# A streaming encoder step: TensorE's static order worked out with nine of its model's latencies changed

## The chip, the cores and the metric

The kernel runs on one core of a Trainium2 chip. The metric is the device time of one execution in microseconds (us). The kernel before took 1478.51 us in the median of three runs (1473.87 to 1479.91). The engines are named as in the profile: PE is TensorE, DVE is VectorE, ACT is ScalarE, POOL is GpSimd, and SP is SyncE, which starts all the DMAs spoken of here.

## The reference

One layer of a streaming encoder for 1024 prompt rows and 32 sample rows, model width 1024, all in 32-bit floats:

```python
xn = rmsnorm(x, pre_norm_g)
u = xn @ w_in                       # gq gk gv gr gg | dq dk dv dg | ma mb
log_a = log_sigmoid(gr @ gla_w_a2 + gla_b_a) / 16
o_gla, state = gla(gq, gk, gv, log_a)            # 4 heads, gated linear attention with a state
y_gla = (rmsnorm(o_gla) * silu(gg)) @ w_proj_gla
o_diff = diff_attend(rope(dq), rope(dk), dv)     # 8 heads, softmax(q1 k1) - lambda * softmax(q2 k2)
y_diff = (rmsnorm(o_diff) * silu(dg)) @ w_proj_diff
y = x + rmsnorm((sigmoid(ma) * y_gla + sigmoid(mb) * y_diff) @ w_out, post_norm_g)
```

Besides y it returns the new keys, values and GLA states. The prompt rows start from nothing; the sample rows attend to 512 past frames and go on from a given GLA state.

## The kernel before

**Products.** Each 32-bit operand is split into a high and a low part, and a product is three matmuls: high by high, high by low, low by high. The projections are lines 486 to 488 (helper `fill`), 464 to 466 (`proj`) and 1122 to 1124 (`pg_first`).

**Stages, in time.** Norm and value projections (to about 220 us); the GLA stage with 4 heads (to about 560); the difference attention with 8 heads (to about 1177); GLA's output projection (to about 1280); that of the difference attention (to about 1373); the last product with `w_out`.

**The order of the work.** In the GLA stage, the difference stage and GLA's output projection TensorE's order is fixed when the program is built. The class `Order` keeps a clock of its own. Each thread of work yields its next step as (cost, needs, banks): what TensorE spends on it, the events it needs with a latency behind each, and the PSUM banks it takes. The first thread in line whose step is ready by the model goes next; the heads' own work stands first, `fill` last. `fill` yields the projections that later heads need, in steps of two k tiles, six matmuls at a modelled cost of 0.9. `S.mark(event)` notes when something was issued, `S.free(tag, latency)` says when a bank comes free again. The latencies are the table `W`:

```python
    def _ready(self, step):
        _, needs, banks = step
        r = max([self.at.get(e, math.inf) + lat for e, lat in needs], default=0.0)
        for tag in set(banks):
            n = banks.count(tag)
            have = sorted(self.banks[tag])
            r = max(r, have[n - 1] if len(have) >= n else math.inf)
        return r
```

If nothing is ready, the model's clock moves on to the first step that will be. At run time nothing is reordered: TensorE works through the fixed order and waits where a step isn't ready. Some `fill` jobs need a result of the head in work (a GLA head's query job waits for the branch of the head before, its key job for the last key transpose of that head, the gate job for that head's output; in the difference stage the query and key jobs wait for the scores of the head before), so there are places where no fill is to be had. The other engines' orders are made by the scheduler from the order of the code.

**The steps spoken of.** In a GLA head: `ps_a` (L579 to L581, eight chunks in two groups of four, in the one bank of tag t, evicted by DVE at L582); `ps_as` (L588 to L590, the sample rows, evicted at L591); a branch on a flag (L600) that all engines take together; then on DVE L643, L637, L644 and L646, which make the decayed keys; `ps_kt` (L654), which transposes them; `pS` and `po` (L700 to L727), the state and the output of each chunk; L181, L182 (POOL) and L733, which normalise a group's output `o_sb`; `ps_y` (L740), its transposes, two for each group, evicted with the gate into `yt` by DVE at L743, and stored from there by SP (L746). `yt` has one buffer.

```python
                yield 0.11 * n, [(("on", h, grp), W["on"]), (("sg", h, e), W["sg"])], ["t"]
                ps = tbank("ps_y")
                ...
                S.free("t", W["y_t"])
```

In the difference stage: `ps_s` (L906, L907) are the scores, from keys `k` and `kl` whose halves are copied by DMA (L862); `ps_t` (L954) transposes the probabilities, split by ACT (L956) and DVE (L957), and `po` (L967 to L969) multiplies them by the values; for the sample rows `ps_st` (L1029) transposes, evicted by ACT (L1031) and DVE (L1032), `po_s` (L1041, L1042) multiplies and is evicted by ACT (L1043), and `ps_so` (L1052) transposes the result. `ps_t`, `ps_st`, `ps_so` share the one bank of tag t, too.

Of the kernel before, what the change touches and what calls it, by code (L numbers as in the profile page):

```python
# [50 lines left out]

W = {
# [3 lines left out]
    "tr_t": 2.27, "dv": 5.65, "at": 2.45, "pv_o": 1.1, "sdg": 1.84, "sdk": 21.35, "kc": 7.45, "ss_s": 3.69,  # L56
    "sp": 7.1, "st_t": 1.14, "sv": 3.44, "spt": 0.43, "so_o": 3.58, "so": 4.1, "so_t": 0.72, "yg0": 4.48,
    "yg": 1.18, "pg_b": 1.72, "sm": 1.98, "sm_w": 0.00141, "sm_s": 2.25, "p": 2.4, "p_w": 0.00204,
}

# [1264 lines left out]
```

## Time and profile before

| | us |
|---|---|
| median of 3 runs | 1478.51 (1473.87 to 1479.91) |
| the profiled execution's own time | 1477.82 |
| its span, first to last instruction | 1476.1 |
| PE busy | 1422.4 (96%) |
| DVE, ACT, POOL busy | 789.9, 600.5, 300.2 |
| granted clock of TensorE, mean | 0.990 |

The profile is of one execution; what lies between its span and its own time (1.7 us) is start and end. Times in rows are from the start of the span. A bracket at the end of a row of the timeline gives the idle time of the engine before that row and what ended it. Matmuls overlap: their durations are longer than the distance from one to the next, so distances are read from start to start.

### The profile page before, as it was taken

The numbers are of one execution on the slowest core, as the hardware profiler recorded it, in microseconds if no ns is written. First come the engines' busy times: TensorE is split into PE (matmuls) and PEld (weight loads), VectorE is DVE, ScalarE is ACT, GpSimd is POOL, SyncE is SP. The second block draws the span as 40 slices with busy tenths as digits, with TensorE's granted clock in tenths as the row PEclk, the third lists the DMA queues.
The fourth block names the chain that finished last, engine by engine and source line by source line (L and its number), as shares of the span: only waits on it lengthen the run. The fifth ranks groups of instructions, "written<-read, shape, count | busy, mean of one in ns | idle before, by whom it ended". The sixth has DMA issues, their size and how long they took to land.

```text
span 1476.1 us, 22367 instructions
## 1 busy us (share of the span) xinstructions
PE 1422.4 (96%) x8848; PEld 1327.5 (90%) x8848; DVE 789.9 (54%) x1464; ACT 600.5 (41%) x1262; POOL 300.2 (20%) x186
## 2 busy tenths in 40 slices
PE   8999999989999999899999999999899899999997
PEld 6787779889999899899989998998899799999997
DVE  5602005756565343576776766678665536455415
ACT  4513114535354233455555555555455432221311
POOL 1200002222223124223222222222221111122001
PEclk9999999999999999999999999999999999999999
DMA  8620111122222233313232332223222278634205
GB/s 303 211 107 31 45 50 50 54 73 73 87 64 86 71 109 110 98 54 116 68 100 69 97 90 93 75 77 90 92 69 80 96 265 306 222 132 132 101 1 193
DMA packets 66742, 156.58 MB, mean 106 GB/s; under 512 B 10008, under 2 KB 28568, under 8 KB 65600
## 3 DMA queue, kind: packets, MB, share of 16 engines
q1 hardware_dynamic: 66624, 155.01, 32.5%
q8 instruction: 74, 1.21, 0.4%
q14 instruction: 44, 0.36, 0.1%
HBM read 104.39 MB, written 40.04 MB: 98 GB/s over the span
## 4 chain that ended last, share of the span: by engine, by line
PE 51%; DVE 6%; DMA 4%; ACT 2%; issue 1%; POOL 1%; SPq 0%; DVEq 0%; POOLq 0%; ACTq 0%
PE ps_w L486 9%; PE ps_w L487 9%; PE ps_w L488 9%; PE ps_w L465 2%; PE ps_w L464 2%; PE ps_w L466 2%; PE ps_s L907 2%; PE ps_t L954 2%; PE ps_s L906 2%; PE ps_c L1216 2%; PE ps_c L1218 2%; PE ps_c L1217 2%; DMA ydr<-ydd 1%; DMA kl<-kl 1%; PE po L968 1%
## 5 line engine op out<-in xcount | busy, mean ns | idle before, releaser
L486 PE MATMUL ps_w<-X,wh 128*128 128x352 f32 x1344 | 452.5, 337 | 1.4 <-DVE vo L292 1.1
L487 PE MATMUL ps_w<-X,wl 128*128 128x352 f32 x1344 | 437.7, 326 | 0.0
L488 PE MATMUL ps_w<-X,wh 128*128 128x352 f32 x1344 | 435.7, 324 | 0.0
L456 POOL TENSOR_TENSOR wl<-wr,wh 128x1024 fp32r<-128x1024 f32 x72 | 180.5, 2507 | 656.3 <-ACT wh L454 493.1
L486 PEld LDWEIGHTS ps_w<-X,wh 128*128 128x128 f32 x1344 | 255.0, 190 | 5.5 <-issue 3.0
L487 PEld LDWEIGHTS ps_w<-X,wl 128*128 128x128 f32 x1344 | 255.4, 190 | 1.2 <-issue 1.2
L488 PEld LDWEIGHTS ps_w<-X,wh 128*128 128x128 f32 x1344 | 254.7, 190 | 0.0
L912 ACT ACTIVATE p<-ps_s,nm 128x256 f32<-128x256 f32 (+7 forms) x128 | 94.6, 741 | 58.8 <-DVE ps_s L908 30.8
L306 PE MATMUL ps_v<-wh,X 128*128 128x512 f32 x248 | 97.6, 394 | 1.2 <-DVE X L245 1.2
L305 PE MATMUL ps_v<-wh,X 128*128 128x512 f32 x248 | 98.5, 397 | 0.2 <-DVE g L343 0.2
L307 PE MATMUL ps_v<-wl,X 128*128 128x512 f32 x248 | 98.3, 396 | 0.0
L454 ACT ACTIVATE wh<-wr 128x1024 fp32r<-128x1024 f32 x72 | 75.9, 1054 | 54.6 <-PE ps_w L488 30.6
L910 DVE TENSOR_REDUCE nm<-ps_s 128x1 f32<-128x256 f32 (+7 forms) x128 | 94.8, 747 | 2.7
L292 DVE TENSOR_TENSOR vo<-ps_v,vo 32x512 f32<-32x512 f32 x4 | 2.7, 678 | 140.8 <-ACT vo L291 140.8
L908 DVE MEMSET ps_s<- 64x64 f32 x128 | 14.3, 112 | 115.9 <-PE ps_s L907 114.3
L671 POOL TENSOR_TENSOR vl<-vr,vh 128x512 fp32r<-128x512 f32 (+1 forms) x20 | 24.6, 1228 | 219.4 <-ACT vh L670 219.4
L906 PE MATMUL ps_s<-k,q 128*128 128x512 f32 (+2 forms) x192 | 68.0, 362 | 1.2 <-DMA k<-k 1.2
L907 PE MATMUL ps_s<-kl,q 128*128 128x512 f32 (+2 forms) x192 | 63.8, 348 | 3.7 <-DMA kl<-kl 3.7
L288 ACT ACTIVATE vo<-ps_v 128x512 f32<-128x512 f32 x32 | 19.1, 595 | 115.1 <-PE ps_v L307 114.7
L956 ACT ACTIVATE ah<-ps_t 128x512 fp32r<-128x512 f32 (+2 forms) x96 | 46.9, 488 | 43.5 <-PE ps_t L954 42.7
L957 DVE TENSOR_TENSOR al<-ps_t,ah 128x512 fp32r<-128x512 f32 (+2 forms) x96 | 53.2, 554 | 18.3 <-ACT ah L956 17.0
L465 PE MATMUL ps_w<-Y,wl 128*128 128x352 f32 x192 | 62.2, 324 | 0.0
(319 smaller groups left out, 2968.8 us busy)
## 6 DMA issues: line engine op xcount, KB each, us to landing
wr<-w SPq DMA_DIRECT2D x72, 512.0 KB
thd<-gate SPq DMA_DIRECT2D x16, 528.0 KB
xn<-xn SPq DMA_DIRECT2D x16, 512.0 KB
wr<-wv SPq DMA_DIRECT2D x16, 512.0 KB
newk<-rr SPq DMA_DIRECT2D x8, 528.0 KB
ygr<-ygd SPq DMA_DIRECT2D x8, 528.0 KB
tha<-thd SPq DMA_DIRECT2D x8, 528.0 KB
ydr<-ydd SPq DMA_DIRECT2D x8, 528.0 KB
```

Source lines behind the costliest of these rows:

```text
L305: mm(ps, xk[:, 0, t0 : t0 + P], wh[:, k, :], start=(k == 0), stop=False)
L306: mm(ps, xk[:, 1, t0 : t0 + P], wh[:, k, :], start=False, stop=False)
L307: mm(ps, xk[:, 0, t0 : t0 + P], wl[:, k, :], start=False, stop=(k == KT - 1))
L456: nc.gpsimd.tensor_tensor(wl, wr, wh.bitcast(F32), op=ALU.subtract)
L465: mm(ps[:, :n], wl[:, k, :], src[k][:, 0, t0 : t0 + n], start=False, stop=False)
L486: mm(ps[:, :n], wh[:, k, :], src[k][:, 0, t0 : t0 + n], start=(k == 0), stop=False)
L487: mm(ps[:, :n], wl[:, k, :], src[k][:, 0, t0 : t0 + n], start=False, stop=False)
L488: mm(ps[:, :n], wh[:, k, :], src[k][:, 1, t0 : t0 + n], start=False, stop=(k == KT - 1))
L906: mm(ps[:, n0 : n0 + n], qs[m][:, qsl], ks[m][:, n0 : n0 + n], start=True, stop=False)
L907: mm(ps[:, n0 : n0 + n], qs[m][:, qsl], kls[m][:, n0 : n0 + n], start=False, stop=True)
L910: ve.tensor_reduce(nm, ps[:, 0:w], axis=AX.X, op=ALU.max, negate=True)
L912: act(p[:, 0:w], ps[:, 0:w], AF.Exp, bias=nm, accum_out=sm[:, m : m + 1])
```

## The change

Nine latencies of the table `W` get other values. No instruction is added or removed; the same steps come in another order on TensorE, and the other engines' orders follow it.

```diff
-    "a_t": 1.14, "as_t": 0.79, "kd": 3.96, "kt_t": 0.3, "kt": 8.05, "v": 3.97, "s_s": 0.37, "st": 1.91,
-    "po_o": 0.67, "sg": 0.65, "on": 6.76, "y_t": 0.64, "pv": 1.41, "m_o": 1.54, "dq": 7.76, "dk": 14.32,
...
+    "a_t": 2.5, "as_t": 0.79, "kd": 5.6, "kt_t": 0.3, "kt": 8.05, "v": 3.97, "s_s": 0.37, "st": 1.91,
+    "po_o": 0.67, "sg": 0.65, "on": 7.8, "y_t": 1.6, "pv": 1.41, "m_o": 1.54, "dq": 18.0, "dk": 19.0,
...
```

In the two lines left out `tr_t` goes from 2.27 to 2.5, `st_t` from 1.14 to 2.6 and `so` from 4.1 to 4.9. `a_t` is how long the bank is taken behind `ps_a`, `y_t` behind `ps_y`, `tr_t` behind `ps_t`, `st_t` behind `ps_st`; `kd` is from the issue of the decayed keys to `ps_kt`, `on` from that of the normalised output to `ps_y`, `dq` and `dk` from the end of a query or key job to the head's first scores, and `so` from the samples' last scaling to `ps_so`.

Three places in the order. First, TensorE where GLA head 0 ends and head 1 begins (`X_88` are the normed rows that the fill jobs read). Before:

```order
L588 MATMUL ps_as<-qh,kh 32x32
L589 MATMUL ps_as<-qh,kl 32x32
L590 MATMUL ps_as<-ql,kh 32x32
L486 MATMUL ps_w<-X_88,wh 128x352
L487 MATMUL ps_w<-X_88,wl 128x352
L488 MATMUL ps_w<-X_88,wh 128x352
L486 MATMUL ps_w<-X_88,wh 128x352
L487 MATMUL ps_w<-X_88,wl 128x352
L488 MATMUL ps_w<-X_88,wh 128x352
L599 TENSOR_LOAD fl
L600 COMPARE_AND_BRANCH
```

After:

```order
L725 MATMUL po<-sh,qh 128x256
L726 MATMUL po<-sh,ql 128x256
L727 MATMUL po<-sl,qh 128x256
L588 MATMUL ps_as<-qh,kh 32x32
L589 MATMUL ps_as<-qh,kl 32x32
L590 MATMUL ps_as<-ql,kh 32x32
L599 TENSOR_LOAD fl
L600 COMPARE_AND_BRANCH
```

Before, behind the last `po` of head 0 came one fill step, a group of `ps_a`, two fill steps, `ps_as`, one step, the branch, two steps, and both `ps_y`. After, the six steps and the group stand ahead of that `po`; `ps_as` follows it at once, the branch `ps_as`, and both `ps_y` the branch. On DVE L181 and L733 have moved behind the branch.

Second, TensorE at the first scores of the difference stage, a piece of the difference (`+` is what stands there now):

```order
+L486 MATMUL ps_w<-X_88,wh 128x352
+L487 MATMUL ps_w<-X_88,wl 128x352
+L488 MATMUL ps_w<-X_88,wh 128x352
+L486 MATMUL ps_w<-X_88,wh 128x352
+L487 MATMUL ps_w<-X_88,wl 128x352
+L488 MATMUL ps_w<-X_88,wh 128x352
 L906 MATMUL ps_s<-k_6794,q_6600 128x128
 L907 MATMUL ps_s<-kl_6796,q_6600 128x128
```

Up to the first `ps_s` 36 matmuls of fill, six steps, have moved ahead; SP's queue has the copies of `k` and `kl` in the same place between the same transfers as before.

Third, TensorE at the end of the difference stage (`po_s` are the samples' products, `po` the last product with the values). Before, one fill step behind the first `ps_st`:

```order
L486 MATMUL ps_w<-X_89,wh 128x352
L487 MATMUL ps_w<-X_89,wl 128x352
L488 MATMUL ps_w<-X_89,wh 128x352
L1029 MATMUL ps_st<-ident,p 32x128
L1041 MATMUL po_s<-vcs,smp 32x128 x4
L1042 MATMUL po_s<-smp 32x128
L954 MATMUL ps_t<-ident,p 128x128 x8
L1041 MATMUL po_s<-vcs,smp 32x128 x4
L1042 MATMUL po_s<-smp 32x128
L967 MATMUL po<-ah,vh 128x256
L968 MATMUL po<-al,vh 128x256
L969 MATMUL po<-ah,vl 128x256
```

After:

```order
L486 MATMUL ps_w<-X_89,wh 128x352
L487 MATMUL ps_w<-X_89,wl 128x352
L488 MATMUL ps_w<-X_89,wh 128x352
L1029 MATMUL ps_st<-ident,p 128x128 x4
L954 MATMUL ps_t<-ident,p 128x128 x8
L967 MATMUL po<-ah,vh 128x256
L968 MATMUL po<-al,vh 128x256
L969 MATMUL po<-ah,vl 128x256
```

Before, a fill step, the second `ps_st` and the first `po_s` group stood between the first `ps_st` and the last two `ps_t` (one row, x8), and the other `po_s` group between these and `po`. After, `ps_st`, both `ps_t` and `po` follow one another; the second `ps_st` comes behind `po`, and both `po_s` groups and `ps_so` come among the matmuls of GLA's output projection.

Elsewhere on TensorE, counted in the two orders: the first of the three `ps_kt` of a head comes one step later behind `ps_as` (two in head 3), the second `ps_st` of a head pair one step later behind the first, a second `ps_y` one step later behind the first in most groups. The first `ps_y` of head 3's last group comes two steps behind its last `po`, where it came six steps behind. The first `ps_a` group of head 1 comes one fill step, one `po` and two `pS` groups (12 small matmuls) behind head 0's fourth `ps_y`, where two more steps and two more groups of each lay between; that of head 2 comes two steps behind head 1's last big `ps_y`, where it came four steps behind. In head 2 the two `ps_y` of the last group follow each other without a step between, where one lay between, with one step ahead of them behind a `ps_a` group and two steps between them and `ps_as`.

More of the change, by code (lines that the diff above doesn't have):

```diff
@@ L53 @@
     "w_pj": 1.5, "z_s": 6.02, "z": 15.1, "a": 0.07, "pf_t": 0.58, "gk": 0.6, "gq": 4.35, "qk": 8.01,
[2 rows of a table removed]
-    "tr_t": 2.27, "dv": 5.65, "at": 2.45, "pv_o": 1.1, "sdg": 1.84, "sdk": 21.35, "kc": 7.45, "ss_s": 3.69,
-    "sp": 7.1, "st_t": 1.14, "sv": 3.44, "spt": 0.43, "so_o": 3.58, "so": 4.1, "so_t": 0.72, "yg0": 4.48,
[2 rows of a table added]
+    "tr_t": 2.5, "dv": 5.65, "at": 2.45, "pv_o": 1.1, "sdg": 1.84, "sdk": 21.35, "kc": 7.45, "ss_s": 3.69,
+    "sp": 7.1, "st_t": 2.6, "sv": 3.44, "spt": 0.43, "so_o": 3.58, "so": 4.9, "so_t": 0.72, "yg0": 4.48,
     "yg": 1.18, "pg_b": 1.72, "sm": 1.98, "sm_w": 0.00141, "sm_s": 2.25, "p": 2.4, "p_w": 0.00204,
```

## The prediction

> **What bounds the kernel now.** I read the busy shares first, then TensorE's waits, then the timeline around each wait.
>
> ```profile
> span 1476.1 us, 22367 instructions
> PE 1422.4 (96%) x8848; PEld 1327.5 (90%) x8848; DVE 789.9 (54%) x1464; ACT 600.5 (41%) x1262; POOL 300.2 (20%) x186
> ```
>
> TensorE is the bound: 1476.1 − 1422.4 = 53.7 us are idle, and the change removes no matmul. So only idle time and clock can move. The waits of TensorE name the idle time that the nine values could touch (columns: us in total, times, longest):
>
> ```profile
> engine line waited for: us in total, times, longest us
> PE ps_y L740 <- DVE yt L743: 5.2, 4, 2.6
> PE ps_kt L654 <- DVE k L646: 4.5, 3, 2.5
> ...
> PE ps_s L907 <- DMA kl<-kl: 3.7, 4, 2.2
> PE ps_st L1029 <- DVE smp L1032: 3.6, 2, 2.3
> ...
> PE pf L550 <- DVE yt L743: 0.7, 1, 0.7
> ```
>
> Each is a step that the model thought ready and that was not. A longer latency puts fill steps ahead of it. A fill step's price, from TensorE's timeline beside one group of transposes (start, duration, line):
>
> ```profile
> 318.99 0.28 PE L727 MATMUL po<-sl,qh 128*128 128x256 f32 x1
> 319.11 0.32 PE L486 MATMUL ps_w<-X,wh 128*128 128x352 f32 x1
> ...
> 320.07 0.22 PE L579 MATMUL ps_a<-qh,kh 128*128 128x128 f32 x1
> ```
>
> From 319.11 to 320.07 one step of six matmuls: 0.96 us, 0.16 us per matmul.
>
> The long waits cost more than their length. The windows' columns are length, PE, PEld, DVE, ACT and POOL busy (count), granted clock, DMA:
>
> ```profile
> core 0: us, PE busy (x) PEld busy (x) DVE busy (x) ACT busy (x) POOL busy (x), PEclk, DMA share, GB/s
> ...
> 500.00:502.00 2.00, 2.00 (x9) 2.00 (x8) 0.81 (x2) 1.06 (x2) 0.00 (x0) 0.50 0.01 3
> ...
> 600.00:605.00 5.00, 5.00 (x19) 5.00 (x19) 1.16 (x4) 0.46 (x2) 0.00 (x0) 0.51 0.01 4
> 605.00:610.00 5.00, 5.00 (x34) 5.00 (x33) 1.80 (x8) 1.87 (x6) 0.00 (x0) 1.00 0.00 0
> ...
> 1036.00:1040.00 4.00, 4.00 (x17) 3.52 (x17) 0.13 (x2) 0.54 (x1) 0.00 (x0) 0.70 0.43 165
> ```
>
> At 0.51 of the clock 19 matmuls ran in 5 us, at full clock 34: 15 too few, 15 x 0.15 = 2.2 us lost after the stall at 598. By the same rate (6.8 per us) 500–502 lost 4.6 matmuls, 0.7 us, and with what is left of that slow stretch on either side about 1.2; 1036–1040 lost 10, 1.5 us.
>
> **What goes.** The stalled steps, from TensorE's timeline, the idle time before each in brackets:
>
> ```profile
> 400.18 0.66 PE L740 MATMUL ps_y<-ident,o_sb 128*128 128x128 f32 x4 [0.79 <-DVE yt L743]
> 419.18 0.28 PE L654 MATMUL ps_kt<-ident,k 128*32 128x128 f32 x1 [1.25 <-DVE k L646]
> 495.67 0.32 PE L488 MATMUL ps_w<-X,wh 128*128 128x352 f32 x1
> 498.48 0.28 PE L654 MATMUL ps_kt<-ident,k 128*32 128x128 f32 x1 [2.49 <-DVE k L646]
> 595.74 0.30 PE L906 MATMUL ps_s<-k,q 128*128 128x128 f32 x1 [1.16 <-DMA k<-k]
> 598.25 0.44 PE L907 MATMUL ps_s<-kl,q 128*128 128x128 f32 x1 [2.21 <-DMA kl<-kl]
> 599.36 0.45 PE L907 MATMUL ps_s<-kl,q 128*128 128x128 f32 x1 [0.45 <-DMA kl<-kl]
> 1034.82 0.27 PE L1029 MATMUL ps_st<-ident,p 128*32 128x128 f32 x1 [2.31 <-DVE smp L1032]
> ```
>
> - kd 3.96 to 5.6: one step more ahead of the three key transposes that wait, two at the last. The three waits are 4.5 − 1.25 − 2.49 = 0.76, 1.25 and 2.49: off come 0.76, 0.96 and 1.9, and with the last the slow clock, 1.2. Together 4.8.
> - dk, dq: the first scores come six steps, 5.8 us, later. Their copies keep their place on SP's queue, so 1.16 + 2.21 + 0.45 = 3.8 go, and 2.2 of clock: 6.0. The other 1.0 of the 3.7 at L907 are later heads and stay.
> - st_t 1.14 to 2.6: one step more before the second sample transpose: 0.96 of each of the two waits (3.6 − 2.31 = 1.3, and 2.31), and 1.5 of clock: 3.4.
> - y_t 0.64 to 1.6: one step more: 0.79 here and the 0.7 at L550: 1.5.
>
> The gaps are counted from the modelled end of the matmul before; from 495.67 + 0.16 to 498.48 it is 2.65, so each stall that vanishes gives 0.16 more: eight, 1.3. Sum removed: 4.8 + 6.0 + 3.4 + 1.5 + 1.3 = 17.0 us.
>
> **What comes.** Fill is not made, it is moved. Where its next job waits for the head in work, fill runs out, and each step spent earlier is missing there. Three such places are in the order: the change of head 0 to 1, the last group of head 3, and the end of the difference stage.
>
> Head 0 to 1: VectorE's and TensorE's timeline, and a row of the view by source on who waits for the branch (us, times):
>
> ```profile
> 315.33 0.75 DVE L743 SCALAR_TENSOR_TENSOR yt<-ps_y,gg_half,sg 128x512 f32<-128x512 f32 x1 [1.68 <-DMA ygd<-yt]
> 321.15 0.65 DVE L181 TENSOR_SCALAR ss<-ss 128x4 f32<-128x4 f32 x1
> 323.03 1.22 DVE L733 TENSOR_TENSOR o_sb<-o_sb,ss 128x1024 f32<-128x1024 f32 x1 [0.91 <-POOL ss L182]
> 324.91 0.20 PE L588 MATMUL ps_as<-qh,kh 128*32 128x32 f32 x1 [1.42 <-DVE ar L582]
> 328.84 1.23 DVE L643 TENSOR_TENSOR b<-b 128x1024 f32<-128x1024 f32 x1 [3.45 <-DVEq L600]
> 329.99 1.31 DVE L637 TENSOR_TENSOR al<-ar,ah 128x1024 fp32r<-128x1024 f32 x2
> 332.11 1.11 PE L740 MATMUL ps_y<-ident,o_sb 128*128 128x128 f32 x4 [2.65 <-DVE yt L743]
> ...
>   DVE b L643: 9.1, 4
> ```
>
> The last po ended at 319.27 and the second ps_y started at 332.11: 12.84 us, which held six fill steps (5.8) and a group L579–L581 (12 matmuls, 1.3 by the 0.11 to 0.12 us from one small matmul to the next, 318.99 to 319.11). After, those 7.1 us of work stand ahead of po; behind it come only ps_as, the branch L600 and both ps_y. VectorE's chain is then in line. ps_as waits 1.2 to 2.0 for L582 (the 1.42 lies between), its own matmuls and L591 take about 0.5, and the branch holds VectorE 3.45 in this head (two of its four waits leave (9.1 − 6.9)/2 = 1.1 for each of the others). Then L181 (0.65), L643 (1.23), L733 (1.22, moved behind the branch), L637 (1.31) and the eviction L743 (0.75). Together 8.0 to 11.1 us from po to the second ps_y. I take 10.3, the shorter wait and this head's own branch: 10.3 + 7.1 − 12.84 = +4.5 (2.2 to 5.4), and 0.5 for a clock that stays low longer: +5.0.
>
> Last group of head 3:
>
> ```profile
> 529.11 0.28 PE L727 MATMUL po<-sl,qh 128*128 128x256 f32 x1
> 532.22 1.23 DVE L733 TENSOR_TENSOR o_sb<-o_sb,ss 128x1024 f32<-128x1024 f32 x1 [1.19 <-POOL ss L182]
> ```
>
> po ends at 529.39, o_sb is there at 533.45: 4.06 us. Six steps (5.8) covered it; two (1.9) are left: +2.1. A gap of that length is near those that lost the clock: +2.5, up to 3.6 with the 1.5 of the window at 1036.
>
> End of the difference stage:
>
> ```profile
> 1166.85 0.60 PE L1029 MATMUL ps_st<-ident,p 128*128 128x128 f32 x4
> 1167.90 0.42 DVE L1032 TENSOR_TENSOR smp<-ps_st,smp 128x256 f32<-128x256 f32 x1 [1.93 <-ACT smp L1031]
> ...
> 1171.98 0.66 PE L954 MATMUL ps_t<-ident,p 128*128 128x128 f32 x4 [1.41 <-DVE al L957]
> 1174.32 0.39 PE L967 MATMUL po<-ah,vh 128*128 128x256 f32 x1 [0.36 <-ACT os__13014 L1043]
> ```
>
> One fill step, another ps_st and both po_s groups stood between these. After, ps_st, two ps_t and po follow one another. The first ps_t waits for L1032, 1168.32 − 1166.85 less its own 0.4: 1.0; the second 1.41 as now; po for its last split, 1174.32 − 1171.98 − 0.4 = 1.9. That is 4.3 where 1.41 + 0.36 = 1.8 were: +2.5, and as they come within some 6 us, the 1.5 of clock: +4.0 (2.5 to 4.7). The two po_s groups move into the next stage, each with an eviction like the 0.36: +0.5.
>
> Three places lost their distance to the one bank t: the L579 group after head 0's fourth ps_y, the next head's group after its last ps_y, and a pair of ps_y in head 2 that now has no fill between. Their eviction can wait for yt's store, since yt has one buffer:
>
> ```profile
> 309.66 0.66 PE L740 MATMUL ps_y<-ident,o_sb 128*128 128x128 f32 x4
> 402.83 0.75 DVE L743 SCALAR_TENSOR_TENSOR yt<-ps_y,gg_half,sg 128x512 f32<-128x512 f32 x1 [2.70 <-DMA ygd<-yt]
> ```
>
> The first eviction (315.33 + 0.75 = 316.08) ended 5.8 us behind its ps_y (310.32). Now 12 small matmuls and one fill step stand there, 1.4 + 0.96 = 2.4: 0 to 3.4, and I take 1.0, as the store's start shifts too. The second ended 403.58 − 400.84 = 2.74 behind; two steps (1.9) are left: +0.8. In the pair the second would wait 0.79 + 0.96 = 1.75 by the row at 400.18, where (5.2 − 2.65 − 0.79)/2 = 0.88 is waited now: +0.9; ps_as stands two steps behind it, +0.8 by the same 2.74; and the pair's first is one step behind a group L579: with 0.3 for that +2.0 (1 to 4).
>
> Sum added: 5.0 + 2.5 + 4.0 + 0.5 + 1.0 + 0.8 + 2.0 = 15.8 us (7.8 with the low ends: 2.2 + 2.1 + 2.5 + 0 + 0 + 0 + 1.0). Net −1.2 on the profiled execution's own 1477.82, that is 1476.6; the median of three, 1478.51, is 0.7 above it. I say **1476**.
>
> **A rule weighed.** The trace: a gap of 2.31 us at 1034.82 was followed by 1036–1040 at 0.70 of the clock. The Trainium skill, "TensorE: Matmul & The Clock Gate", section "HAM oscillation — how this bites in real kernels", asks for no idle gap of TensorE above about 3.4 us, so a shorter one would be free. The trace differs: it lost 1.5 us behind 2.31. By the rule the 4.9 us of clock that I remove would have been no gain of the longer latencies.
>
> **Rivals.** (a) The run-out places are better covered than I read: the added terms fall at their low ends, 7.8. Then 1477.8 − 17.0 + 7.8 = 1469. For it: the branch took little in the other heads, and bank t often comes free early. Against: the distances in the order are plain, and 4.06 and 5.8 us are in the trace. 0.20.
>
> (b) Slower: the one yt buffer. With pairs of ps_y closer, each second eviction waits for the first's store, the one bank t is held for the 5.8 us seen once, and three groups behind it stall: (5.8 − 2.4) + (5.8 − 1.9) + (5.8 − 1.9) = 11.2 for the 3.8 counted, and 1.5 of clock on each: 1476.6 + 7.4 + 4.5 = 1488. It decides when stores land over 5 us late. For it: stores stand in line with weight loads on SP's one queue. Against: of the eviction waits only one was near that. 0.14.
>
> (c) The clock falls only behind gaps over 3.4 us and the slow stretches came from elsewhere: they stay, 4.9 of the gain go, and with them the 0.4 + 1.5 of clock that I added behind short gaps: 1476.6 + 4.9 − 1.9 = 1480. For it: the stretch at 598 began while copies were still landing. Against: each of the three windows of half clock above begins right behind a stall of over 2.2 us. 0.03. The page named above would have it so.
>
> (d) The stalls are real but their releasers move as far as the steps do, so nothing changes: 1478. For it: the order of VectorE, ACT and SP moves as well. Against: the copies of the first scores are released by their own job. 0.05.
>
> **How the numbers follow.** A measurement of this kernel tells about 0.5% (7.4 us) from no change: below 1471.1 is faster, above 1485.9 slower. My forecast (0.58) nearly cancels and lies within, as do (c) and (d): same 0.66. (a) is faster, 0.20; (b) slower, 0.14. The range: the unknown ends of the added terms reach 8 below and some 9 above: 1467 to 1486.
>
> **What would show it.** Right: no wait at the first scores (L906, L907) nor a slow clock behind them; key transposes waiting under 1 us; ps_y behind the branch of head 1 waiting some 5 to 8 us in all; waits of over 4 us at the end of the difference stage; PE busy near 1420 with idle about 50. Wrong: idle below 45, so that the places of running out were covered; or long waits of L579 behind yt's store.

## The result, and the profile after

The changed kernel takes 1501.68 us in the median of six runs (1500.29 to 1505.67), the kernel before 1477.95 in six (1473.87 to 1480.96): ratio 1.0168, interval 1.0152 to 1.0184, so 23.7 us slower. The prediction said 1476 and 1467 to 1486. One execution of all those spoken of here took far longer than the others of its kernel (2414.38 us, in the kernel with the split ranked higher) and is left out of its time and ratio. Its profiled execution took 1504.91, its span is 27.1 us longer than that of before. First the page of the changed kernel, span and busy shares:

```profile
span 1503.2 us, 22365 instructions
PE 1427.4 (95%) x8848; PEld 1329.3 (88%) x8848; DVE 797.6 (53%) x1464; ACT 592.2 (39%) x1262; POOL 307.0 (20%) x186
```

TensorE is idle for 75.8 us where it was 53.7, and its work takes 5.0 us longer at a mean clock of 0.986 (0.990 before). DVE does the same operations in 7.7 us more; that is the first thing that the prediction had no term for.

TensorE's waits after (us in total, times, longest):

```profile
engine line waited for: us in total, times, longest us
PE ps_y L740 <- DVE o_sb L733: 10.8, 2, 8.6
PE ps_t L954 <- DVE al L957: 9.6, 13, 1.8
PE ps_t L954 <- DVE ps_s L908: 5.2, 4, 2.0
PE ps_t L954 <- DVE p L917: 5.1, 5, 1.5
PE ps_st L1029 <- DVE smp L1032: 4.2, 3, 1.4
PE ps_y L740 <- DVE yt L743: 3.2, 4, 0.8
PE ps_as L588 <- DVE yt L743: 2.7, 1, 2.7
```

The first row holds two places that were foreseen: the change of head 0 to 1 (8.6) and the last group of head 3 (2.2). The three rows of `ps_t`, 19.9 us, 13 + 4 + 5 times, are not in the prediction but for one wait of 1.4 us at the end of the stage. The group of all 288 transposes in the kernel before (busy us, mean ns, then the idle time ahead of them and what ended it):

```profile
L954 PE MATMUL ps_t<-ident,p 128*128 128x128 f32 x288 | 47.6, 274 | 7.0 <-DVE al L957 4.1 <-DVE smp L1055 1.7 <-DVE ps_s L908 0.9
```

After, the same group:

```profile
L954 PE MATMUL ps_t<-ident,p 128*128 128x128 f32 x288 | 48.9, 279 | 21.1 <-DVE al L957 9.6 <-DVE ps_s L908 5.2 <-DVE p L917 5.1
```

The idle time ahead of them has tripled. No row of L906 or L907 is left among the waits.

Where in time: windows cut at the same steps in both kernels (first `ps_z`, last `ps_y`, first `ps_s`, last `po` of the difference stage, first step of the next projection). Columns: length, PE, PEld, DVE, ACT and POOL busy (count), granted clock, DMA share, GB/s. Before:

```profile
core 0: us, PE busy (x) PEld busy (x) DVE busy (x) ACT busy (x) POOL busy (x), PEclk, DMA share, GB/s
...
220.80:552.80 332.00, 315.36 (x2039) 303.29 (x2038) 182.77 (x305) 142.12 (x283) 86.97 (x53) 0.99 0.24 74
552.80:595.70 42.90, 41.79 (x261) 41.48 (x259) 16.73 (x25) 15.95 (x30) 16.32 (x7) 1.00 0.43 129
595.70:1177.30 581.60, 565.78 (x3628) 534.93 (x3628) 394.33 (x781) 300.47 (x692) 139.87 (x66) 0.99 0.28 83
1177.30:1280.00 102.70, 98.29 (x582) 94.39 (x583) 51.60 (x54) 33.11 (x35) 16.96 (x7) 0.98 0.76 268
```

After:

```profile
222.20:565.70 343.50, 319.04 (x2051) 307.22 (x2050) 178.37 (x305) 141.11 (x283) 89.12 (x53) 0.97 0.22 72
565.70:611.20 45.50, 45.50 (x286) 45.50 (x285) 16.72 (x25) 16.39 (x31) 17.27 (x7) 1.00 0.48 142
611.20:1199.60 588.40, 559.42 (x3572) 526.67 (x3571) 410.37 (x778) 292.21 (x686) 143.16 (x64) 0.99 0.27 81
1199.60:1306.10 106.50, 101.05 (x603) 96.22 (x602) 44.32 (x53) 31.78 (x36) 17.39 (x8) 0.98 0.71 250
```

The lengths grow by 11.5, 2.6, 6.8 and 3.8 us; 1.4 and 1.0 lie ahead and behind; together 27.1. But the windows don't hold the same work any more: matmuls have moved over the borders, 12 and 25 into the first two, 21 into the last, 56 out of the difference stage. At the 0.16 us of a matmul that the prediction read, the growth at equal work is 9.6, −1.4, 15.8 and 0.4. So the GLA stage (head 0 to 1, and the rest of its places) lost 9.6, and the difference stage 15.8 although its first stall is gone. In that stage PE's idle time went from 15.8 to 29.0, and DVE was busy 16.0 us longer with three instructions fewer.

### The profile page after: what moved, and what is told of

It is laid out like the page before. It is cut to its first block, busy times and chain, and to the rows that moved or that the text cites. A ratio compares the mean times of both kernels' runs of the same rounds, so it can differ in the third digit from the quotient of the medians.

```text
span 1503.2 us, 22365 instructions
## 1 busy us (share of the span) xinstructions
PE 1427.4 (95%) x8848; PEld 1329.3 (88%) x8848; DVE 797.6 (53%) x1464; ACT 592.2 (39%) x1262; POOL 307.0 (20%) x186
## 5 line engine op out<-in xcount | busy, mean ns | idle before, releaser
L486 PE MATMUL ps_w<-X,wh 128*128 128x352 f32 x1344 | 453.0, 337 | 2.1 <-DVE vo L292 1.1
L456 POOL TENSOR_TENSOR wl<-wr,wh 128x1024 fp32r<-128x1024 f32 x72 | 183.1, 2544 | 527.0 <-ACT wh L454 472.3
L486 PEld LDWEIGHTS ps_w<-X,wh 128*128 128x128 f32 x1344 | 255.2, 190 | 7.2 <-issue 3.3
L908 DVE MEMSET ps_s<- 64x64 f32 x128 | 14.1, 112 | 105.7 <-PE ps_s L907 104.6
L954 PE MATMUL ps_t<-ident,p 128*128 128x128 f32 x288 | 48.9, 279 | 21.1 <-DVE al L957 9.6
L957 DVE TENSOR_TENSOR al<-ps_t,ah 128x512 fp32r<-128x512 f32 (+2 forms) x96 | 53.2, 554 | 29.0 <-ACT ah L956 27.8
L906 PE MATMUL ps_s<-k,q 128*128 128x512 f32 (+2 forms) x192 | 67.6, 360 | 0.0
L956 ACT ACTIVATE ah<-ps_t 128x512 fp32r<-128x512 f32 (+2 forms) x96 | 46.8, 487 | 45.8 <-PE ps_t L954 45.6
L907 PE MATMUL ps_s<-kl,q 128*128 128x512 f32 (+2 forms) x192 | 63.2, 346 | 0.0
```

Source lines behind the costliest of these rows:

```text
L456: nc.gpsimd.tensor_tensor(wl, wr, wh.bitcast(F32), op=ALU.subtract)
L486: mm(ps[:, :n], wh[:, k, :], src[k][:, 0, t0 : t0 + n], start=(k == 0), stop=False)
L906: mm(ps[:, n0 : n0 + n], qs[m][:, qsl], ks[m][:, n0 : n0 + n], start=True, stop=False)
L907: mm(ps[:, n0 : n0 + n], qs[m][:, qsl], kls[m][:, n0 : n0 + n], start=False, stop=True)
```

## The experiments

The theory to test was that the later `dq` and `dk` do the harm. They move the first scores six fill steps back, and by that every head stands at another place against the fill jobs. A job here is twelve steps. Counted in the order, in jobs from its start, the first scores of the eight heads stand at

```
before  24.33  28.50  32.50  36.42  40.42  44.58  48.58  52.50
after   24.83  29.00  33.00  36.92  40.92  44.83  48.83  52.75
```

half a job later for heads 0 to 4, a quarter for the others. What a job asks of the other engines, so the theory, then falls beside other steps of the head: the rotation (L825, L827) and the splitting of the keys (L858, L859) on DVE, the splitting of the weights on POOL (L456). The rivals: bank t, held longer by the model's new `tr_t` and `st_t`; fill that is missing at the end; DVE's queue order by itself, which the scheduler makes anew; and POOL and DVE in each other's way.

### The nine values in three parts

The first kernel is before with `"dq": 18.0, "dk": 19.0` and nothing else.

> The kernel before with dq and dk alone set to 18.0 and 19.0. Theory phase: the six steps ahead of the first scores take away the stall there (7 us), but every later head of the difference stage now stands six steps further along the fill jobs, so POOL's weight split (L456) and the jobs' work on VectorE fall beside the softmax and the transposes: 14 to 17 us more waits at ps_t and po, in all 1484 to 1489. Theory bank (the rival: the new waits at ps_t come from tr_t, st_t and so, which place the transposes and the sample steps): only the stall goes, 1469 to 1473.

Measured 1499.23 against 1478.80, ratio 1.0122 (1.0091 to 1.0152): the sign is the theory's, the size 10 us above its range. The second has the four of the GLA stage alone, `"a_t": 2.5, "kd": 5.6, "on": 7.8, "y_t": 1.6`.

> The kernel before with a_t, kd, on and y_t alone changed. Theory phase: the GLA stage gets about 10 us longer as in the changed kernel, the first scores still stall, and the difference stage, whose order against the fill jobs is that of before, stays within 3 us: 1486 to 1490. Rival (what the GLA stage leaves behind disturbs the difference stage): the 17 us at ps_t come too, 1500 to 1506.

Measured 1489.31, ratio 1.0068 (1.0049 to 1.0088). The third has the rest, `"tr_t": 2.5, "st_t": 2.6, "so": 4.9`.

> The kernel before with tr_t, st_t and so alone changed. Theory phase: the end of the difference stage is 4 us longer, GLA's output projection 2, the two sample waits 3 shorter; the heads are shifted by at most two steps, so that up to 6 us come at ps_t: 1480 to 1487. Theory bank: most of the 17 us at ps_t are here: 1495 to 1499.

Measured 1476.45, ratio 0.9984 (0.9970 to 0.9998), below what was expected. With 0.0122 + 0.0068 − 0.0016 = 0.0174 the three parts add up to the whole 0.0168. So the theory that put the loss on bank t falls: those values are worth a little gain. `dq` and `dk`, whose stall was to give 6.0 us, carry the larger part of the loss. The waits of the kernel with `dq` and `dk` alone show the three rows of `ps_t` again:

```profile
PE ps_t L954 <- DVE al L957: 9.4, 13, 1.8
...
PE ps_t L954 <- DVE ps_s L908: 5.2, 4, 2.0
PE ps_t L954 <- DVE p L917: 5.1, 5, 1.5
```

### Other places of the heads

Before with `"dk": 16` (two steps later) and with `"dk": 24` (eleven steps, 0.92 of a job):

> The kernel before with dk alone set to 16.0: two steps more ahead of the first scores, the heads at 0.50, 0.67, 0.67, 0.58, 0.58, 0.50, 0.50, 0.42 of a fill job. Theory phase: close to before's place in the job, and 2 of the 7 us of the first stall gone with perhaps its slow clock: 1471 to 1478. Rival fill: a third of what dq and dk cost, 1481 to 1486.

> The kernel before with dk alone set to 24.0: the first scores come eleven steps later instead of six, and the heads start at 0.25, 0.42, 0.50, 0.42, 0.50, 0.17, 0.08, 0.00 of a fill job, where before has 0.33, 0.50, 0.50, 0.42, 0.42, 0.58, 0.58, 0.50 and dk 19.0 has 0.83, 0.00, 0.00, 0.92, 0.92, 0.83, 0.83, 0.75. Theory phase (where in a fill job a head stands decides): no stall at the first scores, the first five heads like before, the last three with the waits of dk 19.0: 1474 to 1484. Rival fill (fill spent ahead of the scores is missing in the heads): worse than dk 19.0, 1500 to 1508.

Measured 1493.71, ratio 1.0119 (1.0102 to 1.0136), and 1514.10, ratio 1.0246 (1.0228 to 1.0264). Both are above every expectation. That two steps cost about as much as six, and that almost a whole job is the worst, contradicts the theory as it was put, by the fraction of a job. With `dk` at 24 the first five heads meet the jobs at nearly the same fraction (the last three half a job later), but it is another kind of job (query, key and gate jobs take turns), and these five take 74.5 to 83.3 us, where 69.0 to 74.8 were. The waits of this kernel say what that does:

```profile
PE ps_w L486 <- ACT rr L829: 13.6, 4, 3.5
```

The fill itself waits, in a row that the waits of before don't have. What it waits for is its bank `ps_w`, which ACT empties into `rr` (L829), and of `rr` there is one buffer. At the first of the four places the last key split that reads `rr` (L859) ended at 663.39, and then ACT went on:

```profile
663.48 0.82 ACT L829 ACTIVATE rr<-ps_w 128x352 f32<-128x352 f32 x2 [3.64 <-issue]
```

In the changed kernel the row of L486 and `rr` holds only 0.8 us, so this kernel pays for its place in another way. The new form of the theory: kind and fraction both count. It can be tested, since a gate job can be moved so that the same jobs lie beside the heads again:

```diff
-GATES_DIFF = [2, 1, 1, 1, 1, 1, 1, 2, 2]
+GATES_DIFF = [3, 1, 1, 1, 1, 1, 1, 2, 1]
-    ... "dk": 14.32,
+    ... "dk": 24,
```

> The kernel before with dk at 24.0 and one gate job of the fill moved from the end of the difference stage to its start, so that the heads start at 24.25, 28.50, 32.42, 36.58, 40.58, 44.50, 48.50 and 52.50 jobs once the added one is taken off, where before has 24.33, 28.50, 32.50, 36.42, 40.42, 44.58, 48.58 and 52.50. Theory place (which job's work on VectorE and POOL falls beside which block of a head decides): the heads wait as before within 6 us, the first scores don't stall (7 us less), the end of the stage has a job less of fill (12 more): 1477 to 1487. Rival (scores that come later cost as such, by fill that is missing): 1498 to 1515.

Measured 1480.99, ratio 1.0024 (1.0012 to 1.0037), 33 us below the same `dk` without the moved job. In its order the first scores stand at 25.25, 29.50, 33.42, 37.58, 41.58, 45.50, 49.50 and 53.50: one job later than before, within one step for six heads and two steps for the other two. The difference stage with `dk` at 24 (columns as above), first with the gate job where it was:

```profile
603.30:1213.80 610.50, 572.20 (x3564) 534.89 (x3562) 390.11 (x781) 292.08 (x689) 142.70 (x65) 0.96 0.26 78
```

and with it moved:

```profile
603.10:1177.20 574.10, 554.96 (x3564) 521.32 (x3562) 393.61 (x781) 297.82 (x689) 137.69 (x65) 0.99 0.28 82
```

The first scores start at the same time and the stage has the same 3564 matmuls, but takes 36.4 us less: its idle time is 19.1 instead of 38.3, and the rest is matmuls at a clock of 0.99 instead of 0.96. So a later start by itself, or fill spent early, doesn't make the loss of this kernel: with the moved job a whole job was spent early, too. It doesn't gain anything either, though the stall at the first scores is gone: the waits for `kl` fall only to 1.5 us, and the last head has a job less to fill with.

For the changed kernel itself the traces can be set side by side by head. Heads 1, 3 and 5 hold the same 288 matmuls of fill and 164 others in every kernel below (head 1 with the moved job six fewer). Given are the head's place in jobs (with the moved job one is taken off) and the time from its first scores to those of the next head, in us:

| | before | `tr_t`, `st_t`, `so` | `dk` 16 | `dk` 24, moved job | changed |
|---|---|---|---|---|---|
| head 1 | 28.50: 69.0 | 28.50: 69.1 | 28.67: 75.4 | 28.50: 70.5 | 29.00: 74.7 |
| head 3 | 36.42: 70.9 | 36.58: 70.9 | 36.58: 70.9 | 36.58: 70.6 | 36.92: 75.6 |
| head 5 | 44.58: 70.8 | 44.50: 69.1 | 44.50: 69.1 | 44.50: 69.1 | 44.83: 74.0 |

At one and the same place a head takes the same time within 1.5 us in these kernels, and at the changed kernel's places it takes 3.2 to 5.7 us more. This also says where the two steps of `dk` 16 cost: in head 1 (6.4) and head 2 (79.6 where 74.7 were), while head 3, moved by the same two steps, takes no longer. The kernel with the moved job has heads 1 and 2 in place or one step early, so it never met the two costly places.

### DVE's and ACT's queues by themselves

Two kernels are the changed one with TensorE's order untouched and the work of DVE and ACT for `ps_t` given a higher rank in the scheduler. In the first, the split of the transposes (L956, L957):

```diff
+ with tc.high_priority(offset=1300): act(ah[...], pv, AF.Copy)
+ with tc.high_priority(offset=1300): ve.tensor_tensor(al[...], pv, ah[...], ...)
```

> The changed kernel with its order on TensorE word for word, and the splits of the transposed probabilities (L956 on ACT, L957 on VectorE) given a higher priority, so that the fill job's key splits, gates and rotations no longer stand ahead of them there. Theory order (bank t comes free late since L957 stands behind other work on VectorE): the waits of ps_t for L957, 9.6 us, fall to about 4, and 5 to 10 us come back: 1491 to 1497. Theory port alone (what is late is lengthened, not badly placed): within 4 us of the changed kernel, 1498 to 1505.

Measured 1517.31, ratio 1.0265 (1.0244 to 1.0285): about 14 us above the changed kernel by the ratios, and above both expectations. In the second the softmax too (L908 to L917):

> The changed kernel with its order on TensorE word for word, and on VectorE and ACT the whole softmax of the heads (L908 to L917) and the splits L956, L957 raised together, so that a fill job's gates, rotations and key splits stand behind them. Splits raised alone had cost 17 us, since the softmax fell behind. Theory order (fill's work stands ahead of the chain that feeds the transposes): 5 to 12 us come back, 1489 to 1497. Rival (the waits are meetings at the shared port, and any order has its own): 1499 to 1512.

Measured 1510.19, ratio 1.0219 (1.0197 to 1.0241), within what the rival said. The waits of the first:

```profile
PE ps_t L954 <- DVE p L917: 15.7, 8, 3.6
...
PE ps_t L954 <- DVE r L1021: 6.1, 2, 3.5
...
PE ps_t L954 <- DVE al L957: 1.9, 2, 1.4
```

The wait for L957 did fall, from 9.6 to 1.9 us, and the waits for the softmax (L917) and the samples' softmax (L1021) took its place. The order of these two queues is worth some 14 us at one and the same order of TensorE, so it counts; but a better rank for the split, which was to give the loss back, made it larger. That the queues' order alone makes the loss of the change is not shown: neither rank gave any of it back.

### POOL in DVE's way

The trace of the changed kernel shows DVE instructions that last two to six times as long as elsewhere. DVE's timeline (start, duration, line):

```profile
817.14 0.55 DVE L957 TENSOR_TENSOR al<-ps_t,ah 128x384 fp32r<-128x384 f32 x1
817.61 3.15 DVE L917 SCALAR_TENSOR_TENSOR p<-p,sm 128x1024 f32<-128x1024 f32 x1
```

POOL's at that time:

```profile
817.25 2.43 POOL L456 TENSOR_TENSOR wl<-wr,wh 128x1024 fp32r<-128x1024 f32 x1
```

TensorE's:

```profile
820.90 0.63 PE L954 MATMUL ps_t<-ident,p 128*128 128x128 f32 x4 [1.51 <-DVE p L917]
```

and the same step of before, on DVE:

```profile
800.76 1.28 DVE L917 SCALAR_TENSOR_TENSOR p<-p,sm 128x1024 f32<-128x1024 f32 x1
```

L917 ends at 820.76, 1.08 us behind the end of POOL's split (819.68): nearly its whole work comes after it. The transposes wait 1.51 us. Over the run the groups of L916 show it (busy us, mean ns). After:

```profile
L916 DVE TENSOR_SCALAR p<-p,sm,neglam 128x128 f32<-128x128 f32 (+3 forms) x64 | 54.6, 854 | 1.6
```

before:

```profile
L916 DVE TENSOR_SCALAR p<-p,sm,neglam 128x128 f32<-128x128 f32 (+3 forms) x64 | 40.9, 638 | 1.8
```

That is 13.7 us on one line, for the same 64 instructions; the group of L917 took 2.7 us less (55.9 where 58.6 were), so such meetings moved as well as grew. To size POOL's part, POOL's split was cut into four pieces, so that one piece holds DVE for a shorter time (0.87 us in the mean of the changed kernel, the whole 2.54). First everywhere, in the changed kernel and in the kernel before:

```diff
-nc.gpsimd.tensor_tensor(wl, wr, wh.bitcast(F32), op=ALU.subtract)
+for k in range(0, KT, 2): nc.gpsimd.tensor_tensor(wl[:, k : k + 2], wr[:, k : k + 2], ...)
```

> The changed kernel with each weight split on POOL (L456, 128x1024, 2.4 us) cut into four of 128x256. Theory port: VectorE's L916 and key splits, when they start beside that instruction, last until it ends (2.2 to 3 us where 0.6 to 0.8 is usual), and the transposes wait for them; in quarters the hold is about 0.6 us, so 8 to 14 us of the 24 come back: 1487 to 1494. Rival (the waits come from the order on VectorE itself, in which the splits of a fill job stand ahead of those of the transposes): unchanged within 4 us, 1498 to 1506.

> The kernel before with the same cut of POOL's weight split. Theory port: fewer such meetings here, so only 0 to 5 us come back: 1473 to 1479. Rival: the same, 1475 to 1481; what tells is the difference to the changed kernel with the cut, 10 to 16 us by the port and 24 by the rival.

Measured 1503.60, ratio 1.0182 (1.0165 to 1.0199), which is the rival's range, and 1488.04, ratio 1.0070 (1.0050 to 1.0090), above both ranges. The pair says that the cut itself costs the kernel before 11 us, and that it narrows the distance between the two; as a test of the size it is muddled. So the cut was made in the difference stage alone, in both:

> The changed kernel with POOL's weight split cut into four in the difference stage alone (cut everywhere, it took 11 us off that stage and gave 8 back in the others). Theory port: those 11 us come off and nothing is given back, 1489 to 1494. Rival (the cut helped by another order on VectorE, which the scheduler made for it): within 4 us of the changed kernel, 1498 to 1504.

> The kernel before with POOL's weight split cut into four in the difference stage alone. Theory port: the 3 us that the cut took off this stage when it was made everywhere, 1473 to 1477; beside the changed kernel with the same cut this leaves a difference of 17 to 20 where 24 were. Rival: 1477 to 1481.

Measured 1493.28, ratio 1.0103 (1.0087 to 1.0120), and 1474.58, ratio 0.9976 (0.9965 to 0.9987). The group of `ps_t` in the changed kernel with the cut:

```profile
L954 PE MATMUL ps_t<-ident,p 128*128 128x128 f32 x288 | 48.7, 278 | 11.9 <-DVE al L957 8.2 <-DVE p L917 1.3 <-DVE ps_s L908 1.2
```

The waits for L917 fall from 5.1 to 1.3 us, those for L908 from 5.2 to 1.2, those for L957 hardly. With the cut on both sides 1.0103 / 0.9976 = 1.0127 of the 1.0168 are left. POOL's part of the change is so about 0.004, 6 us (2 to 10 by the intervals). The profiled executions put it higher: the difference stage of the changed kernel falls from 588.4 to 577.7 us with the cut, that of the kernel before stays (581.5 and 582.2), but these single executions lie up to 4 us above their kernels' medians. By head the cut says what is POOL's. Heads 1, 3 and 5 of the changed kernel take 73.2, 71.2 and 71.1 us with it, those of the kernel before 69.1, 70.9 and 70.4: in heads 3 and 5 the loss is all but gone, in head 1 four of its 5.7 us stay. The cut and the third part of the values together:

> The kernel before with tr_t, st_t and so changed and POOL's weight split cut into four in the difference stage. If the two gains add (2.4 us of the three values, 3 us that the cut took off that stage of the kernel before): 1470 to 1474. If they meet in the same waits: 1475 to 1478.

Measured 1474.15, ratio 0.9986 (0.9971 to 1.0001). Two versions beat both kernels: the cut in the difference stage (0.9976) and `tr_t`, `st_t`, `so` alone (0.9984), each by less than 0.5%, and together they give no more than one of them.

### The GLA values one by one

Before with `"kd": 5.6` alone, with `"a_t": 2.5` alone, with `"on": 7.8` alone:

> The kernel before with kd alone at 5.6: one more fill step ahead of the key transposes, two in head 3. By the term of the prediction 4.8 us go (0.8 and 1.0 and 1.9 of the waits, 1.2 of slow clock), and the step missing ahead of the last group of head 3 costs nothing, as five steps still cover it: 1472 to 1475. Rival (what is spent there is missing at once elsewhere, or the other engines' orders shift): 1477 to 1482.

> The kernel before with a_t alone at 2.5. In its order both ps_y at the change of GLA head 0 to 1 follow the branch with no fill between, as in the changed kernel, while the last group of head 3 keeps five steps. Theory (fill spent between two ps_a groups is what is missing there): the GLA stage gets 5 to 8 us longer at that one place, 1482 to 1487. Rival (it takes all four values together): 1477 to 1480.

> The kernel before with on alone at 7.8: one step more ahead of the first ps_y of most groups, and both places above keep their fill. Theory: nothing waits there now and nothing is late, so 1476 to 1480. Rival (each step put ahead is paid back where fill runs out): 1481 to 1485.

Measured 1480.15, ratio 1.0012 (0.9999 to 1.0025); 1490.02, ratio 1.0099 (1.0068 to 1.0129); 1483.47, ratio 1.0057 (1.0037 to 1.0077). The first and the third are where the rivals had them, the second lies 3 us above its theory. With `kd` alone the key transposes wait 0.8 us for L646 where they waited 4.5, and the time is the same:

```profile
PE ps_y L740 <- DVE yt L743: 7.2, 6, 2.5
...
PE pf L550 <- DVE yt L743: 3.4, 2, 2.3
```

5.2 and 0.7 us stood there before: the 3.7 us of the keys came back as 4.7 us behind the one buffer `yt`, in steps that the fill had covered. With `a_t` alone one `ps_y` waits 4.1 us behind the branch of head 1, and the keys and `pf` wait 2.8 and 2.9 us more. The single values don't add up: about 2, 15 and 8 us for three of the four, 10 for all four (`y_t` alone was not run). Each moves the places of the others, so a value has no price of its own here.

## Why the prediction was wrong

**The step that failed** is "dk, dq: the first scores come six steps, 5.8 us, later … off come 6.0", together with "Three such places are in the order". The stall did go: TensorE was busy for all 45.50 us of the window ahead of the first scores, and the scores started without a wait:

```profile
611.24 0.27 PE L907 MATMUL ps_s<-kl,q 128*128 128x128 f32 x1
```

But the six steps were costed as fill that is only missing where fill runs out. They also shift all eight heads against the fill jobs, and a fill job isn't only matmuls. Its DVE and POOL work, which had a good place in the kernel before, fell beside the last blocks' softmax and transposes. This was costed at nothing and is the largest term: 15.8 us at equal work in the stage, of which some 3 are for its end (3.3 us of waits where 1.8 were, and 1.6 us more for the last `po` group at the slow clock), and that although the 4.9 us of stall and slow clock at its start (2.21 + 0.45 + 2.2) are gone. The two values alone, which were to gain 6.0, cost 18 by their ratio. That it is the place of the heads against the jobs is shown twice: in the kernel with `dk` at 24, whose own waits are others, 33 of 37 us are gone with the place restored; and in the table by head the same work takes the same time at the same place, and 13.6 us more in heads 1, 3 and 5 at the places of the changed kernel. Head 4 is 1.5 us longer with three fill steps less. Heads 2 and 6, with as many matmuls as before, lost nothing. In heads 3 and 5 what the place brings is POOL's hold on DVE: the cut of POOL's split takes 4.4 and 2.9 us off them.

A second, smaller step is the GLA stage. The prediction's terms for it add up to +4.4 (11.3 come: 5.0, 2.5, 1.0, 0.8 and 2.0; 6.9 go: 4.8, 1.5 and 0.16 for each of four stalls). Measured are 9.6 at equal work, and 10 with the four values alone. The last step of the sum was loose as well: a net of −1.2 gives 1476.6 for the profiled execution and 1477.3 for the median, not 1476.

How a block pays for it, in one case, on DVE:

```profile
739.87 1.27 DVE L917 SCALAR_TENSOR_TENSOR p<-p,sm 128x1024 f32<-128x1024 f32 x1
741.06 2.64 DVE L858 TENSOR_TENSOR kl<-rr,k 64x256 fp32r<-64x256 f32 x1
743.71 0.42 DVE L859 TENSOR_TENSOR kl<-rr,k 64x256 fp32r<-64x256 f32 x1
...
744.59 0.42 DVE L859 TENSOR_TENSOR kl<-rr,k 64x256 fp32r<-64x256 f32 x1
...
747.46 0.68 DVE L957 TENSOR_TENSOR al<-ps_t,ah 128x512 fp32r<-128x512 f32 x1
```

on ACT:

```profile
745.10 0.46 ACT L829 ACTIVATE rr<-ps_w 128x352 f32<-128x352 f32 x1 [4.92 <-issue]
...
746.51 0.59 ACT L956 ACTIVATE ah<-ps_t 128x512 fp32r<-128x512 f32 x1
```

and on TensorE:

```profile
742.73 0.60 PE L954 MATMUL ps_t<-ident,p 128*128 128x128 f32 x4
748.19 0.96 PE L954 MATMUL ps_t<-ident,p 128*128 128x128 f32 x4 [1.36 <-DVE al L957]
```

The transposes issued at 742.73 were done by 743.4, but their split L957 stands in DVE's queue behind four key splits, the first of them held by POOL, and the samples' softmax; it starts at 747.46, and the next `ps_t`, in the same bank, waits. ACT is late, too, and L957 needs its half of the split (L956). ACT stood idle for 4.92 us ahead of L829, the next job's eviction into the one buffer `rr`, until 0.09 us behind the last key split, which reads `rr`; L956, whose transposes were done by 743.4, stands behind that in ACT's queue and starts at 746.51. Such a stand of ACT behind the key splits is there once in the kernel before (3.7 us) and in six heads of the changed one (28.6 us together), and with `dq` and `dk` alone as well. It isn't the price by itself: with POOL's cut 24.1 us of it stay in the same six heads, and heads 3 and 5 lose less than 1 us then. What it is worth in head 1 was not tested.

**Rival (d)** said in passing that "the order of VectorE, ACT and SP moves as well", and took this for a reason why nothing would change. It was the right observation with the wrong price. No rival put a loss in the middle of the difference stage. Of the prediction's own signs, the first scores came as said and the key transposes nearly; idle time is 75.8 us where about 50 was named. Rival (b), the one buffer of `yt`, forecast the sign; its own place gave one wait of 2.7 us and is not the cause.

**The places of running out** were right in kind. Head 0 to 1, TensorE's timeline:

```profile
326.92 0.38 PE L727 MATMUL po<-sl,qh 128*128 128x256 f32 x1 [0.91 <-DVE sl L716]
...
336.72 1.11 PE L740 MATMUL ps_y<-ident,o_sb 128*128 128x128 f32 x4 [8.60 <-DVE o_sb L733]
338.68 1.11 PE L740 MATMUL ps_y<-ident,o_sb 128*128 128x128 f32 x4 [0.85 <-DVE yt L743]
```

From the end of `po` (327.30) to the second `ps_y` 11.4 us went by, just above the range of 8.0 to 11.1 from which 10.3 was taken: the branch held DVE 4.58 us in this execution, not 3.45. In the last group of head 3, `ps_y` waited 2.22 us where 2.1 was said. A slow clock goes with both, as was said (0.50 from 338 to 342 and from 548 to 550). Mis-sized was `ps_as` in a later head, counted at 0.8: it waits the 2.7 us (2.68 in the timeline) of the list above, and a stretch at half clock follows.

At the end of the difference stage:

```profile
1191.00 0.66 PE L1029 MATMUL ps_st<-ident,p 128*128 128x128 f32 x4 [0.97 <-DVE al L957]
1192.59 0.66 PE L954 MATMUL ps_t<-ident,p 128*128 128x128 f32 x4 [0.93 <-DVE smp L1032]
1194.66 0.66 PE L954 MATMUL ps_t<-ident,p 128*128 128x128 f32 x4 [1.41 <-DVE al L957]
```

The two of `ps_t` are as said (1.0 and 1.41); that of `ps_st` was not foreseen, and the 1.9 ahead of the last `po` did not come. The 5 us from 1195 ran at 0.66 of the clock, as was said.

**The removed waits** went as said for the first scores and in the main for the keys (0.9 us left of 4.5 at L646 in the changed kernel, but 2.1 at the same step behind L657, where 0.8 were). The second sample transpose did not keep its gain: `ps_st` waits 4.2 us in three places of the changed kernel, 3.6 in two before. In the kernel with `tr_t`, `st_t` and `so` alone it is 1.4 in one place, so by itself that term gave 2.2 us of waits where 1.9 were said, and it was lost again with the moved heads (with `dq` and `dk` alone `ps_st` waits 8.0 us in four places). And the GLA gains were paid back: the experiment with `kd` alone gave none of its 4.8.

**What stays open.** POOL's hold on DVE makes the loss of heads 3 and 5, and of the whole change 6 us by the medians. How the rest, head 1's above all, divides between DVE's order, ACT's stand behind `rr` and the bank t wasn't told apart; a second buffer for `rr` was not tried. The two experiments on the order only show that the queues can move the time by some 14 us. Which places are costly is seen in the heads' times, but why wasn't worked out from the queues, nor is it explained why the GLA values don't add up beyond the two waits named.

## What to carry to other kernels

When a static order moves one thread of work against another, cost what the moved steps make the other engines do, not only the matmuls: list for one head what each engine's queue holds between two steps that depend on it, before and after. A gain at a single stall is had once, while a shift against a periodic background can be paid in every period, here in four of eight heads. Look for single buffers that pass from one job to the next (`rr` here): an engine that stands behind one holds up all that follows in its queue. And a latency in such a model is also a knob on all the places behind it: try values one at a time, and in pairs, since neither the sign nor the sum follows from the stall that a value was read from.

## What was not expected of the hardware

**A shared port.** In these rows a VectorE instruction with its operands in SBUF that starts while POOL's 128x1024 subtraction runs ends only after it: L917 took 3.15 us instead of 1.28, L858 2.64 instead of 0.42. The one that comes first is not held: L917 at 739.87 lasted 1.27 although POOL's split began at 740.26, and that split took 3.16 us instead of 2.43. L957, with one operand in PSUM, ran from 817.14 for its usual 0.55, and POOL's, which began beside it at 817.25, took its usual 2.43. The Trainium skill, "SBUF — State Buffer", section "Who interferes with whom", says that a VectorE instruction with two SBUF inputs, or in a mode that uses both ports, contends with GpSimd for one shared pair, that the first to start holds it for the whole instruction, and that the other is fully blocked. The rows agree with it.

**The cut has a price.** Four POOL instructions of a quarter the size cost the kernel before 11 us when made in all stages, and gained 3.5 us by the ratio when made in the difference stage alone. In the profiles the price lies ahead of the first scores of the difference stage: they start at 607.8 us with the cut everywhere, at 595.7 without it.

**The clock behind short gaps.** The wait of 2.22 us in head 3 was followed by a stretch at half clock (columns as above):

```profile
548.00:550.00 2.00, 2.00 (x12) 2.00 (x11) 0.56 (x2) 0.42 (x1) 0.00 (x0) 0.50 0.88 245
```

12 matmuls ran in 2 us, all of them busy: they start 0.21 us apart, where the same ones from 550.55 on start 0.12 apart, which would be some 17. The wait of 2.68 us ahead of 500.73 was followed by 0.50 from 504 to 506, and the three waits of 0.93 to 1.41 us at the end of the difference stage by the 0.66 from 1195 to 1200. In this trace TensorE need not stand still for long at once; that the idle time is the cause is read from the order in time alone.
